# The per-layer embedding projections moved to the head of the first stage, and its small loads to GpSimd's queue

## The chip, the cores and the metric

The kernel runs on one core of a Trainium2 chip. The metric is the device time of one execution in microseconds. The core has five engines that each work through an instruction list of their own in order: PE (matrix products), DVE (vector), ACT (scalar), POOL (GpSimd) and SP (which only issues transfers). An instruction that has to wait for another engine or for a transfer holds everything behind it on its own engine. Transfers can be issued by SP, ACT and POOL.

## What is computed

Eleven stages in one launch, on 256 tokens of 1024 channels: an RWKV-7 mixer, an embedding gate, differential attention, a second embedding gate, a norm, then feed-forward, Mamba-2 and sliding-window layers. The change is in the first stage and in the preparation of the two embedding gates. Cut to these:

```python
h = x
# stage 1
hn = rms_norm(h, rw_norm);  dx = token_shift(hn) - hn
r, k, v, gate = ((hn + dx * mu[q]) @ w_in[q] for q in range(4))   # four 1024x1024 products
w_log = f(w0 + tanh((hn + dx * mu[4]) @ w1) @ w2)                 # low rank: w1 is 1024x64
a     = sigmoid(a0 + ((hn + dx * mu[5]) @ a1) @ a2)               # low rank: a1 is 1024x64
# delta rule over 256 tokens, 16 heads of 64; group norm with ln_w, ln_b; bonus; silu(gate)
h = h + y @ w_out
# stage 2 (and 4, with i = 1)
h = h + sigmoid(rms_norm(h, pe_norm[0]) @ pe_w_gate[0]) * (p[0] @ pe_w_proj[0])  # p[i]: 256x256, pe_w_proj[i]: 256x1024
```

The product `p[i] @ pe_w_proj[i]` depends on inputs alone, so it can be made at any time before its gate.

## The kernel before

Every float32 product is made as three: each operand is split into an upper part (a cast to a rounded float32, on ACT) and a lower part (the rest, a subtraction on DVE), and PE multiplies upper by upper, lower by upper and upper by lower. For weights, `wload` (L346) loads a block on SP's queue into a buffer `wr`, casts it into `wh` and subtracts into `wl`. There are few buffers, so that a later load waits for an earlier subtraction.

The first stage, `rwkv`, begins with `load_x` (L296), the sum of squares of the input on ACT, its root by POOL (`rsqrt`, L234), the normed input `hn` in four tiles on DVE (L213), and 16 transposes of it on PE (L229), whose results ACT evicts, scaled, into the tiles `hT`. The difference to the token before is `dx`. `mix` makes the operand of one projection from the two. Then come the value projection (8 blocks of weights) and beside it `lora`, the first low-rank products: they multiply `hT` and `dx` by the tile `wa`, which two transfers on POOL's queue fill (L934, from `rw_w1` and `rw_a1`), and by `wm`, which DVE makes from `wa`.

After the projections a scan works through four groups of four heads (`stream`): `pre` (decay, rate, keys), `scores`, `solve` and `post` (group norm, bonus, gate, and the transposes of the result). For each group `rows` (L709) loads five vectors and `pre` four small pieces of `rw_w2`, `rw_w0`, `rw_a2` and `rw_a0` (L720, L721), all on ACT's queue. Beside the groups run other pieces of work that fill PE: the gate projection, the output projection's halves `l0` and `l1` as far as groups are ready, and, from turn `FP` = 50 on, `ple_proj(0)` and `ple_proj(1)`, the two embedding projections. Each of these loads `p[i]` and transposes it, loads four blocks of 256 columns of `pe_w_proj[i]`, makes 12 products per block on PE, 96 in all for both, evicts each block on ACT and stores it to device memory from POOL's queue (L566). The tiles that hold the stored blocks are called `pp`; the stage `ple` loads them again.

The order of the instructions on each engine is set by a list scheduler that works from the program's order and the dependences. `late` keeps an instruction behind what its engine was given earlier in the program.

Of the kernel before, what the change touches and what calls it, by code (L numbers as in the profile page):

```python
# [8 lines left out]
F32 = mybir.dt.float32  # L9
# [12 lines left out]
NREF = 1  # refinements of the triangular solve  # L22
# banks of PSUM for short and for long use
# [12 lines left out]
# columns of the constant block  # L36
# [3 lines left out]
def constants():  # L40
    """Masks, the identity, rotary angles and distance buckets: from the shapes alone."""
# [18 lines left out]
    # reversed distance vector: column m holds the distance 255 - m; row 32 the mask outside the window  # L60
# [14 lines left out]
def weave(*gens):  # L75
    """Trace the generators by turns, a step each."""
    gens = list(gens)
    while gens:
        for g in list(gens):
            try:  # L80
                next(g)
            except StopIteration:
                gens.remove(g)
# [13 lines left out]
def par(*gens):  # L97
    """The generators by turns, as one generator."""
# [10 lines left out]
def spread(n, m, gen):  # L109
    """The generator's n steps over m turns."""  # L110
# [10 lines left out]
def spaced(n, *gens):  # L121
    """The generators one after another, n turns between."""
# [6 lines left out]
def when(cond, gen):  # L129
    """The generator, from the step on at which its condition holds."""  # L130
    while not cond():
        yield
    yield from gen
# [8 lines left out]
class Net:  # L142
    def __init__(self, ctx, tc, I, out, cst, dbg=None):
# [12 lines left out]
        self.ctx = ctx  # L156
        self.prologue(cst)
# [12 lines left out]
    def m(self, shape, dt=F32, tag="m", bufs=24):  # L170
        """Small tiles: those without a tag outlive a stage, the others do not."""
# [45 lines left out]
    def masked(self, out, a, b, least, init=3.0e38):  # L217
        """out = -(a + b), and its least element, not above init."""
# [12 lines left out]
    def rsqrt(self, out, a, scale, eps):  # L231
        """out = (a * scale + eps) ** -0.5"""
# [4 lines left out]
    def bc(self, vec, n):  # L237
        """A DRAM vector on every partition."""
# [7 lines left out]
    def late(self, ins):  # L246
        """Not before what its engine was given earlier: for loads and constants that need not be early."""
        self.tc.keep_in_program_order(ins)

# [1 line left out]
    def prologue(self, cst):  # L251
# [4 lines left out]
        nc.scalar.dma_start(self.cst, cst[:, :C_KEEP])  # L256
# [5 lines left out]
        # short vectors, on every partition  # L262
# [10 lines left out]

    def first_cols(self, names, queue):
        """Per-channel vectors, channels onto partitions."""
# [16 lines left out]
    def load_x(self, tile, early=False):  # L292
        """The input, as the residual so far."""
# [9 lines left out]
    def load_vec(self):  # L303
        for name, o in self.vec.items():
            self.nc.sync.dma_start(o, self.bc(self.I[name], o.shape[1]))
# [6 lines left out]
    def more_cols(self):  # L312
# [14 lines left out]
        # the gain of the final norm and of the first feed-forward norm after it  # L327
# [9 lines left out]
    def wload(self, W, k0, kn, n0, nn):  # L337
        """[128, kn, nn] of W as an upper and a lower part that sum to it exactly."""
# [12 lines left out]
        self.sub(l, r, h.bitcast(F32))  # L351
# [24 lines left out]
    def linear_cm_g(self, xT, K, W, n0, nn, evac):  # L376
        """The product with channels on partitions: evac takes two tiles of 128 channels by 256 tokens."""
# [16 lines left out]
    def linear2_g(self, xT, K, W, n0, evac):  # L394
        """256 columns, both token tiles side by side."""
# [22 lines left out]
    def split_g(self, src, ks, gains, outs):  # L418
        """src(t, k): [128 tokens, 128 channels]; appends channel-major pairs per gain."""
# [32 lines left out]
    def rstd(self):  # L452
        """Per-token 1/rms of the residual, [128, 2]."""
# [8 lines left out]
    def begin(self, gains):  # L462
        """The stage's input: per-token 1/rms and the residual, channel-major, times each gain."""
# [5 lines left out]
    def finish(self, l0, l1, gains):  # L469
        """The residual's two halves, and the next stage's input on the way."""  # L470
# [33 lines left out]
    def ffn(self, i, j, nxt, kv=False):  # L504
# [7 lines left out]
        def row():  # L512
            """1/rms as a row, on every partition."""
# [39 lines left out]
    def ple_proj(self, i):  # L553
        """p @ w_proj, kept in DRAM until its gate is known."""
# [35 lines left out]
    def final_norm(self):  # L590
        """The residual becomes its norm; what follows takes the operand from before it, the norm's
        gain and per-token factor folded in."""
# [959 lines left out]
```

## Time and profile before

| | us |
|---|---|
| three runs | 1570.53, 1572.88, 1576.21 |
| median | 1572.88 |
| span of the profiled execution, first to last instruction | 1568.3 |
| PE busy in it | 1525.5 |
| DVE busy | 1065.5 |
| ACT busy | 815.9 |
| POOL busy | 77.5 |

The profiled execution's own time is not given apart from its span; the span is 4.6 us below the median of the three runs, which is what lies around it and the difference between runs. Busy PE is modelled from its instructions' starts, so that a stretch that reads 100% busy can still hold gaps of a few per cent. A row of the timeline is: start in us, duration in us, engine, line, operation, result and operands, count, and in brackets the idle time before it with what ended it. Engine names with a q are the part of an engine that issues transfers.

### The profile page before, as it was taken

Reading aid. Unit: us, or ns where it says so; the run is one execution under the profiler, and the core shown is the slowest. Engines: PE = TensorE matmul, PEld = TensorE weight load, DVE = VectorE, ACT = ScalarE, POOL = GpSimd, SP = SyncE. Lnnn points to the kernel's source line nnn. Section 1 sums busy time; section 2 is a strip of 40 time slices with the busy share of each in tenths; the row PEclk is TensorE's granted clock in tenths of the full one; section 3 lists DMA queues with packets and bytes.
Section 4 is the critical chain, followed back from the end, with each engine's and each line's share of the span. In section 5 each row is a group of like instructions: output and inputs, shape, how many; then the busy total and the mean of one; then the engine's idle time right before and its main releaser. Section 6 shows DMA issues by size and latency. Waiting matters only on the chain.

```text
span 1568.3 us, 25792 instructions
## 1 busy us (share of the span) xinstructions
PE 1525.5 (97%) x10164; PEld 1349.5 (86%) x10164; DVE 1065.5 (68%) x1796; ACT 815.9 (52%) x1374; POOL 77.5 (5%) x79
## 2 busy tenths in 40 slices
PE   4999999999899999999999999999999999999998
PEld 4988988777678999887777899998999987799987
DVE  6887777876587756559877756665665657666563
ACT  3546546554466544447666744444544445654342
POOL 0000001111200000000000000000000002000000
PEclk9999999999999999999999999999999999999999
DMA  7421224566946554664442555465554653255463
GB/s 206 139 78 57 73 78 145 181 203 156 248 137 202 181 194 135 229 190 136 121 121 95 178 174 193 154 230 172 165 192 157 229 189 119 85 185 166 159 213 107
DMA packets 145500, 249.88 MB, mean 159 GB/s; under 512 B 11161, under 2 KB 42921, under 8 KB 145380
## 3 DMA queue, kind: packets, MB, share of 16 engines
q1 hardware_dynamic: 138420, 233.87, 46.4%
q0 software_dynamic: 3200, 10.81, 3.3%
q10 hardware_dynamic: 3760, 3.58, 0.9%
q8 instruction: 79, 1.29, 0.3%
q14 instruction: 41, 0.34, 0.1%
HBM read 242.16 MB, written 6.29 MB: 158 GB/s over the span
## 4 chain that ended last, share of the span: by engine, by line
PE 90%; DVE 4%; DMA 2%; ACT 2%; POOL 1%; issue 1%; ACTq 0%; POOLq 0%; DVEq 0%
PE pl L226 73%; PE ps L226 13%; PE ps L229 3%; DMA wr<-in_da_w_in_dram 1%; DVE wl L197 1%; DVE s L197 1%; DMA wa<-in_rw_w_dram 1%; DVE ac L209 1%; ACT s L223 0%; POOL s L993 0%; DVE s L209 0%; POOL m L234 0%; ACT h L223 0%; DMA wr<-in_rw_w_in_dram 0%; DMA base<-in_constants_dram 0%
## 5 line engine op out<-in xcount | busy, mean ns | idle before, releaser
L226 PE MATMUL pl<-wh,s 128*128 128x512 f32 (+1 forms) x2336 | 681.2, 370 | 6.2 <-ACT wh L223 3.2
L197 DVE TENSOR_TENSOR wl<-wr,wh 128x1024 fp32r<-128x1024 f32 (+1 forms) x460 | 528.5, 1173 | 123.0 <-ACT wh L223 121.7
L223 ACT ACTIVATE wh<-wr 128x1024 fp32r<-128x1024 f32 (+1 forms) x460 | 451.1, 1012 | 171.8 <-PE pl L226 103.3
L226 PE MATMUL pl<-s,wh 128*128 128x256 f32 x2816 | 509.1, 283 | 0.0
L226 PEld LDWEIGHTS pl<-wh,s 128*128 128x128 f32 x2336 | 422.3, 189 | 77.8 <-ACT wh L223 6.4
L226 PEld LDWEIGHTS pl<-s,wh 128*128 128x128 f32 x2816 | 439.5, 192 | 0.2
L226 PE MATMUL pl<-wl,s 128*128 128x512 f32 (+1 forms) x1168 | 430.2, 369 | 2.1 <-DVE wl L197 2.1
L226 PE MATMUL pl<-s,wl 128*128 128x256 f32 x1408 | 398.5, 283 | 0.0
L226 PEld LDWEIGHTS pl<-s,wl 128*128 128x128 f32 x1408 | 270.2, 192 | 0.0
L226 PEld LDWEIGHTS pl<-wl,s 128*128 128x128 f32 x1168 | 221.5, 190 | 36.0 <-DVE wl L197 3.3
L223 ACT ACTIVATE s<-s 128x512 f32<-128x512 f32 (+2 forms) x97 | 61.0, 629 | 209.7 <-DVE s L197 209.7
L197 DVE TENSOR_TENSOR s<-pl,s 128x512 f32<-128x512 f32 x44 | 30.4, 691 | 93.7 <-PE pl L226 93.7
L197 DVE TENSOR_TENSOR s<-pl,R 128x512 f32<-128x512 f32 x44 | 30.3, 691 | 82.8 <-PE pl L226 82.6
L234 POOL TENSOR_TENSOR m<-m,base 128x2 f32<-128x2 f32 (+2 forms) x25 | 24.2, 970 | 1006.9 <-DVE m L215 1006.9
L223 ACT ACTIVATE h<-ps 128x512 f16<-128x512 f32 x88 | 48.1, 600 | 36.9 <-PE ps L226 36.8
L223 ACT ACTIVATE s<-ps,base 128x256 fp32r<-128x256 f32 (+1 forms) x104 | 45.7, 471 | 25.0 <-PE ps L229 16.2
L209 DVE SCALAR_TENSOR_TENSOR s<-ps,base,s 128x256 fp32r<-128x256 f32 x96 | 43.6, 479 | 7.2 <-ACT s L223 6.1
L223 ACT ACTIVATE junk<-H 128x512 bf16<-128x512 f32 x40 | 25.1, 627 | 43.6 <-DVE H L209 29.2
L209 DVE SCALAR_TENSOR_TENSOR s<-s,s 128x512 f32<-128x512 f32 x56 | 38.4, 685 | 10.1 <-ACT s L223 9.4
L209 DVE SCALAR_TENSOR_TENSOR H<-pl,m,H 128x512 f32<-128x512 f32 x16 | 12.0, 751 | 47.1 <-PE pl L226 47.1
L226 PE MATMUL ps<-h,h 128*128 128x128 f16 x544 | 42.7, 220 | 1.3 <-ACT h L223 1.2
L226 PEld LDWEIGHTS <-h 128*128 128x128 f16 x576 | 34.9, 99 | 8.4 <-issue 4.8
(229 smaller groups left out, 1324.9 us busy)
## 6 DMA issues: line engine op xcount, KB each, us to landing
wr<-in_ffn_w_dram SPq DMA_DIRECT2D x248, 512.0 KB, 4.6
wr<-in_ssm_w_in_dram SPq DMA_DIRECT2D x40, 512.0 KB, 4.5
wr<-in_rw_w_in_dram SPq DMA_DIRECT2D x32, 512.0 KB, 4.7
wr<-in_da_w_in_dram SPq DMA_DIRECT2D x32, 512.0 KB, 4.7
wr<-in_pe_w_gate_dram SPq DMA_DIRECT2D x16, 512.0 KB, 4.3
wr<-in_ffn_w_dram SPq DMA_DIRECT2D x32, 256.0 KB, 3.1
wr<-in_ssm_w_out_dram SPq DMA_DIRECT2D x16, 512.0 KB, 3.8
wr<-in_rw_w_out_dram SPq DMA_DIRECT2D x8, 512.0 KB, 6.6
```

Source lines behind the costliest of these rows:

```text
L197: self.V.tensor_tensor(out=out, in0=a, in1=b, op=op)
L209: self.V.scalar_tensor_tensor(out=out, in0=a, scalar=sc, in1=b, op0=op0, op1=op1, **k)
L223: self.A.activation(out, a, f, **k)
L226: self.T.matmul(out, l, r, start=start, stop=stop)
L229: self.T.transpose(out, a, self.ident)
L234: self.G.tensor_tensor(out=out, in0=out, in1=self.mhalf[:, :out.free_size()].rearrange("p (a b) -> p a b", a=out.shape[1]) if len(out.shap ...
```

## The change

The two embedding projections are traced at the start of `rwkv`, right after `hn` and before its transposes, and no longer in the scan; the first four of their subtractions are kept in program order (`pin`). `rows` and the small pieces in `pre` are loaded on POOL's queue instead of ACT's. The eleven short vectors (`load_vec`) go from SP's queue to POOL's. The constants that are loaded first are half as many columns (384 instead of 768 of the block `base`), and the rest, with the level masks `lev`, is loaded on POOL's queue after `mix` of the values. The two multiplications that make `wm` are kept in program order.

```diff
 def prologue(self, cst):
-        nc.scalar.dma_start(self.cst, cst[:, :C_KEEP])
+        nc.scalar.dma_start(self.cst[:, :C_CAUS], cst[:, :C_CAUS])
...
+    def more_constants(self):
+        self.late(self.G.dma_start(self.cst[:, C_CAUS:], self.cdram[:, C_CAUS:C_KEEP]))
...
 def load_vec(self):
-            self.nc.sync.dma_start(o, self.bc(self.I[name], o.shape[1]))
+            self.late(self.G.dma_start(o, self.bc(self.I[name], o.shape[1])))
...
 def wload(self, W, k0, kn, n0, nn):
-        self.sub(l, r, h.bitcast(F32))
+        ins = self.V.tensor_tensor(out=l, in0=r, in1=h.bitcast(F32), op=ALU.subtract)
+        if self.pin:
+            self.pin -= 1
+            self.late(ins)
...
 def rwkv(self, nxt):
-        self.G.dma_start(lev[:, :7], self.cdram[:, C_LEV:C_LEV + 7 * P].rearrange("p (a b) -> p a b", a=7))
...
                 self.ts(o[:], self.H[t, f], r[:, t:t + 1], ALU.mult)
+
+        self.pin = 4
+        weave(self.ple_proj(0), self.ple_proj(1))
         for k0 in range(0, 8, 2):
...
         def lora():
-                self.mul(wm[:, :, q], wa[:, :, q], ...)
+                self.late(self.V.tensor_tensor(out=wm[:, :, q], in0=wa[:, :, q], ..., op=ALU.mult))
...
         def rows(tag, names, g):
-                nc.scalar.dma_start(o[:, j], ...)
+                self.G.dma_start(o[:, j], ...)
...
         def pre(g):
-                nc.scalar.dma_start(w2[at:at + 64, q], I[m][0, :, g * 256:(g + 1) * 256])
-                nc.scalar.dma_start(w2[one:one + 1, q], I[c0][:, g * 256:(g + 1) * 256])
+                self.G.dma_start(w2[at:at + 64, q], I[m][0, :, g * 256:(g + 1) * 256])
+                self.G.dma_start(w2[one:one + 1, q], I[c0][:, g * 256:(g + 1) * 256])
...
         weave(mix(2, *xv))
+        self.late(self.G.dma_start(lev[:, :7], ...))
+        self.more_constants()
...
         weave(after(FH, residual()), after(FG[0], spaced(FG[1], *[gate(g) for g in range(4)])),
-              after(FP, chain(self.ple_proj(0), self.ple_proj(1))), when(done(OP[0]), ...),
+              when(done(OP[0]), ...),
```

What this does to the order is seen in three places. The first is POOL's list at the start. Before, the two loads into `wa` stand right behind the root of the norm (the operation on the tile `m_22`):

```order
L628 DMA lev_8_95<-in_constants_dram 128x896
L234 ISA
L234 TENSOR_TENSOR m_22_114<-m_22_114,base_1_72 128x2
L934 DMA wa_6_91<-in_rw_w1_dram 128x8x64
L934 DMA wa_6_91<-in_rw_a1_dram 128x8x64
L283 DMA s_113_562<-in_da_norm_dram 8x128
```

After, the same stretch of POOL's list, from the root on:

```order
L235 TENSOR_TENSOR m_22_113<-m_22_113,base_1_72 128x2
L574 DMA pp0_147<-s_43_187 128x512
L574 DMA pp1_161<-s_48_203 128x512
L574 DMA pp0_147<-s_53_231 128x512
L574 DMA pp1_161<-s_58_247 128x512
L574 DMA pp0_147<-s_63_275 128x512
L574 DMA pp1_161<-s_68_291 128x512
L574 DMA pp0_147<-s_73_319 128x512
L574 DMA pp1_161<-s_74_322 128x512
L944 DMA wa_6_91<-in_rw_w1_dram 128x8x64
L944 DMA wa_6_91<-in_rw_a1_dram 128x8x64
L946 DMA lev_8_95<-in_constants_dram 128x896
```

The eight stores of the embedding projections, each of which waits for the eviction of its block, now stand between the root and the two loads into `wa`.

The second place is ACT's list behind the embedding projections. The tiles `s_68`, `s_73` and `s_74` are the last three evicted blocks, `s_9` to `s_12` are `hT`, and `s_81` is the first operand of the value projection. After:

```order
L224 ACTIVATE s_68_291<-pl_59_250 128x512
L224 ACTIVATE wh_94_400<-wr_93_399 128x1024
L224 ACTIVATE s_73_319<-pl_64_278 128x512
L224 ACTIVATE s_74_322<-pl_69_294 128x512
L224 ACTIVATE s_9_96<-ps_75_325,base_1_72 128x256 x2
L224 ACTIVATE wh_98_441<-wr_97_440 128x1024
L224 ACTIVATE s_10_97<-ps_76_334,base_1_72 128x256 x2
L224 ACTIVATE wh_103_484<-wr_102_483 128x1024
L224 ACTIVATE s_11_98<-ps_77_343,base_1_72 128x256 x2
L224 ACTIVATE s_12_99<-ps_78_352,base_1_72 128x256 x2
L224 ACTIVATE s_81_367<-b_80_364 128x512
```

Every eviction of `hT` now stands behind the last eviction of the embedding projections. On PE, 7 of the 96 embedding products stand ahead of the 16 transposes of `hn`, one among them and 88 behind them; behind those stands the first product with `wa`, ahead of the first value product:

```order
L227 MATMUL pl_69_294<-wh_71_296,s_33_143 128x256
L227 MATMUL pl_69_294<-wl_72_297,s_33_143 128x256
L227 MATMUL pl_69_294<-wh_71_296,s_34_144 128x256
L227 MATMUL ps_96_419<-s_9_96,wa_6_91 128x256
L227 MATMUL pl_92_398<-wh_94_400,s_81_367 128x256
```

The third place is the end of the scan on PE: the last products of the delta rule (`sa` by `GB`, and `S` by `qr`) and the transposes of the last group's result (`ps_851`). Before, 28 products of the output projection stand between the two; the first and the last of them are shown here with their neighbours:

```order
L226 MATMUL ps_841_3637<-S_31_162,qr_597_2700 128x128
L226 MATMUL ps_841_3637<-sa_840_3635,GB_636_2855 128x64 x2
L226 MATMUL pl_831_3601<-wl_844_3647,s_626_2823 128x512
L226 MATMUL pl_831_3601<-wh_843_3646,s_627_2824 128x512
L226 MATMUL pl_832_3602<-wh_843_3646,s_626_2823 128x512
```

```order
L226 MATMUL pl_814_3526<-wh_855_3707,s_810_3503 128x512
L226 MATMUL pl_815_3527<-wh_855_3707,s_809_3502 128x512
L226 MATMUL pl_815_3527<-wl_856_3708,s_809_3502 128x512
L229 MATMUL ps_851_3691<-base_1_72,s_798_3465 128x128 x4
L226 MATMUL pl_815_3527<-wh_855_3707,s_810_3503 128x512
```

After, none stands between them:

```order
L227 MATMUL pl_816_3531<-wh_855_3708,s_810_3512 128x512
L227 MATMUL pl_816_3531<-wl_856_3709,s_810_3512 128x512
L227 MATMUL pl_816_3531<-wh_855_3708,s_811_3513 128x512
L227 MATMUL ps_841_3638<-sa_840_3636,GB_676_3031 128x64 x2
L227 MATMUL ps_841_3638<-S_79_361,qr_645_2901 128x128
L227 MATMUL ps_841_3638<-sa_840_3636,GB_676_3031 128x64 x2
L230 MATMUL ps_851_3692<-base_1_72,s_804_3491 128x128 x4
L227 MATMUL pl_815_3530<-wh_858_3726,s_852_3697 128x512
```

These 28 products, and 4 that stood behind the transposes, moved up into the scan, to where the embedding products had been. From the start of the second stage on, PE's order is the same in both kernels.

## Rows read from the trace of the kernel before

**Rows 1.** The page: busy time with share and instructions, and the chain by engine

```profile
PE 1525.5 (97%) x10164; PEld 1349.5 (86%) x10164; DVE 1065.5 (68%) x1796; ACT 815.9 (52%) x1374; POOL 77.5 (5%) x79
...
PE 90%; DVE 4%; DMA 2%; ACT 2%; POOL 1%; issue 1%; ACTq 0%; POOLq 0%; DVEq 0%
```

**Rows 2.** Windows: busy us (instructions) of each engine, granted clock, DMA share, GB/s

```profile
20.00:30.00 10.00, 5.04 (x27) 4.89 (x28) 7.90 (x19) 3.77 (x9) 0.00 (x0) 0.66 0.62 179
...
200.00:250.00 50.00, 49.86 (x440) 43.52 (x439) 38.04 (x75) 26.27 (x49) 2.82 (x3) 1.00 0.26 86
250.00:290.00 40.00, 37.67 (x360) 33.97 (x360) 31.12 (x57) 25.25 (x45) 4.96 (x7) 1.00 0.40 131
```

**Rows 3.** Timeline of all engines from 13 to 25 us

```profile
13.74 1.03 POOL L934 DMA_DIRECT2D wa<-in_rw_w_dram  x1
...
13.81 2.29 DVE L213 TENSOR_SCALAR b<-x,m 128x512 f32<-128x512 f32 x4 [0.84 <-POOL m L234]
...
14.77 1.10 POOL L934 DMA_DIRECT2D wa<-in_rw_a_dram  x1
...
15.05 3.45 PE L229 MATMUL ps<-base,b 128*128 128x128 f32 x15 [0.23 <-DVE b L213]
...
16.39 2.20 ACTq L709 DMA_DIRECT2D row<-in_rw_r_k_dram  x1
...
20.82 1.57 ACT L223 ACTIVATE s<-ps,base 128x256 f32<-128x256 f32 x4 [0.70 <-DMA row<-in_rw_k_k_dram]
...
24.28 0.63 ACT L223 ACTIVATE s<-b 128x512 fp32r<-128x512 f32 x1 [1.90 <-DVE b L209]
...
24.96 1.19 PE L226 MATMUL ps<-s,wa 128*128 128x256 f32 x2 [6.46 <-ACT s L223]
```

**Rows 4.** Timeline of PE, two pairs of neighbouring 128x256 products after its restart

```profile
26.38 0.41 PE L226 MATMUL pl<-wh,s 128*128 128x256 f32 x1
26.59 0.41 PE L226 MATMUL pl<-wl,s 128*128 128x256 f32 x1
...
28.67 0.28 PE L226 MATMUL pl<-wl,s 128*128 128x256 f32 x1
28.79 0.28 PE L226 MATMUL pl<-wh,s 128*128 128x256 f32 x1
```

**Rows 5.** DMA issues: count, KB of each, median us from issue to landing

```profile
pp<-s POOLq DMA_DIRECT2D x8, 256.0 KB, 2.3
...
wa<-in_rw_w_dram POOLq DMA_DIRECT2D x1, 256.0 KB, 8.3
wa<-in_rw_a_dram POOLq DMA_DIRECT2D x1, 256.0 KB, 10.1
```

**Rows 6.** Groups by form, 195 to 290 us: busy us, mean ns, idle before

```profile
L223 ACT ACTIVATE wh<-wr 128x1024 fp32r<-128x1024 f32 x7 | 7.4, 1059 | 1.6 <-PE pl L226 1.6
L223 ACT ACTIVATE s<-pl 128x512 f32<-128x512 f32 x10 | 6.1, 606 | 2.2 <-PE pl L226 2.1
...
L566 POOL DMA_DIRECT2D pp<-s x8 | 4.5, 560 | 44.7 <-ACT s L223 37.6 <-ACT sa L223 7.1
```

**Rows 7.** Two of the lines' issues on ACT's queue: ns minimum/median/maximum, first and last start

```profile
L709 ACTq DMA_DIRECT2D row<-in_rw_k_k_dram x4: 334/355/366, 14.3 to 164.7; - x4
...
L720 ACTq DMA_DIRECT2D w<-in_rw_w_dram x4: 472/478/529, 2.2 to 119.2; - x4
```

**Rows 8.** Timeline of the end of the scan, 291 to 301 us

```profile
291.57 0.56 PE L226 MATMUL ps<-sa,GB 128*128 128x64 f32 x4
...
293.29 0.69 DVE L919 TENSOR_REDUCE m<-b 128x8 f32<-128x512 f32 x1 [0.70 <-ACT b L223]
...
294.33 1.67 POOL L234 TENSOR_TENSOR m<-m,base 128x8 f32<-128x8 f32 x1 [10.94 <-DVE m L215]
...
296.14 0.39 PE L226 MATMUL pl<-wl,s 128*128 128x512 f32 x1
...
296.82 0.39 PE L226 MATMUL pl<-wl,s 128*128 128x512 f32 x1
...
299.22 0.69 DVE L209 SCALAR_TENSOR_TENSOR s<-s,s 128x512 f32<-128x512 f32 x1
...
300.06 0.63 PE L229 MATMUL ps<-base,s 128*128 128x128 f32 x4 [1.50 <-DVE s L209]
```

More of the change, by code (lines that the diff above doesn't have):

```diff
@@ L156, in __init__ @@
         self.ctx = ctx
+        self.pin = 0
         self.prologue(cst)
@@ L673, in lora @@
             for q in range(2):
-                self.mul(wm[:, :, q], wa[:, :, q], self.colt[:, at + q * 8:at + q * 8 + 8].unsqueeze(2).broadcast_to([P, 8, 64]))
+                self.late(self.V.tensor_tensor(out=wm[:, :, q], in0=wa[:, :, q], in1=self.colt[:, at + q * 8:at + q * 8 + 8].unsqueeze(2).broadcast_to([P, 8, 64]), op=ALU.mult))
             ps = self.pq()
@@ L708, in rows @@
                 a = I[n]
-                nc.scalar.dma_start(o[:, j], bass.AP(tensor=a.tensor, offset=a.offset + g * 256, ap=[[0, P], [1, 256]]))
+                self.G.dma_start(o[:, j], bass.AP(tensor=a.tensor, offset=a.offset + g * 256, ap=[[0, P], [1, 256]]))
             return o
@@ L935, in rwkv @@
         weave(mix(2, *xv))
+        self.late(self.G.dma_start(lev[:, :7], self.cdram[:, C_LEV:C_LEV + 7 * P].rearrange("p (a b) -> p a b", a=7)))
+        self.more_constants()
         self.V.memset(state[:], 0.0)
@@ L951, in rwkv @@
         weave(after(FH, residual()), after(FG[0], spaced(FG[1], *[gate(g) for g in range(4)])),
-              after(FP, chain(self.ple_proj(0), self.ple_proj(1))), when(done(OP[0]), after(OP[1], chain(take(l0, OP[2]), take(l1, OP[3])))),
+              when(done(OP[0]), after(OP[1], chain(take(l0, OP[2]), take(l1, OP[3])))),
               *[after(n, stream(g)) for g, n in enumerate(ST)])
```

## The prediction, made before the changed kernel was run

> **What bounds the kernel now.** I read the page's busy times first, then its chain of waits, then windows of the two stretches that the change touches, and last the timeline at their edges. PE is busy for 97% of the span and carries 90% of the chain [rows 1], so work that leaves PE's list is worth its time on PE, provided nothing else ends later there. That holds in the scan: PE is busy for 49.86 of the 50 us from 200 to 250 and for 37.67 of the 40 us from 250 to 290 [rows 2], and the embedding projections lie there. The one long hole is at the start: the transposes of the normed input end at 18.5, and PE then stands idle for 6.46 us until 24.96 [rows 3]. The change puts the embedding products ahead of that hole. The question is whether they fill it, or whether what PE waits for in the hole is pushed back by them.
>
> What PE waits for has two strands. One is the operand: hn (DVE, from 13.81), transposes to 18.5, evictions into hT on ACT, the difference and the mix on DVE, the cast on ACT from 24.28 to 24.91. The other is the pair of loads into wa: issued at 13.74 and 14.77 [rows 3], landing 8.3 and 10.1 later [rows 5], so at 22.0 and 24.9. Both strands end at 24.9, and the profile names only one of them.
>
> **The start, after.** In PE's new list 88 of the 96 embedding products stand behind the transposes of hn, and hn needs the whole input. Neighbouring 128x256 products start 0.12 us apart at full clock and 0.21 us apart at half clock [rows 4]. If the transposes end at 18.5 as before, the last embedding product ends at 18.5 + 88 x 0.12 = 29.1 and its eviction (0.61, [rows 6]) at 29.7. The input shares its queue with fewer constants at first, so hn may come some 2 us earlier; I take the last eviction at 29, and 27 as the early end. The late end is half clock: 18.5 + 88 x 0.21 + 0.6 = 37.6. The granted clock was 0.66 on the mean from 20 to 30 us [rows 2], the 1.2 GHz level after the idle stretch; with products to run there is no such stretch, so I take full clock.
>
> From the last eviction both strands begin again. The operand: ACT's list has eight evictions into hT behind it (four took 1.57, so 3.1 in all), two casts of weights (1.06 each, [rows 6]) and the cast of the first mix (0.63) [rows 3]: 5.9 us, with DVE's share inside. The first value product therefore starts no earlier than 27 + 5.9 = 32.9, and at 34.9 from the middle value. The loads into wa: they stand behind all eight stores on POOL's list. The last store is issued at the last eviction plus 0.56 [rows 6], the two loads take 1.03 and 1.10 to issue [rows 3], so the second is issued at 29 + 0.56 + 1.03 = 30.6. Its landing is bounded by 2.3 us (256 KB stored from POOL's queue) and 10.1 us (the same load at the start, when the DMA engines were full) [rows 5]: 32.9 to 40.7. The weights of the value projection load in the same stretch, into buffers that come free late, so neither end fits; I take the middle, 6 us, and 36.6. Since the first product with wa stands ahead of the first value product on PE, all value work waits for the later of 34.9 and 36.6. PE restarts 11.7 us later than at 24.96, and what follows, up to the scan, is the same work. **Term 1: +11.7**, from +8 (operand, early) to +15.7 (loads, slow).
>
> A rule speaks for the lower end. The Trainium skill, DMA: Bandwidth & Descriptors, section "Anatomy of one DMA — SWDGE (gpsimd) path", gives a transfer from GpSimd's queue a fixed cost of about 2.0 us plus bytes over 436 GB/s, thus an estimate of 2.6 us for 256 KB. The stores agree with it (2.3), the loads into wa do not (8.3 and 10.1) [rows 5]. By it the second load lands at 33.2, the operand at 34.9 decides, and the sum is 1.7 us lower.
>
> **The scan, after.** It loses 96 x 0.12 = 11.5 us of products and about 1 us of transposes on PE, 12.5 in all; the 8 casts, 8 subtractions and 8 evictions go as well, on engines that wait for PE here. It gains 32 products of the output projection: 28 that stood ahead of the last transposes, and 4 behind them. Three such products start 0.68 us apart [rows 8], so 0.227 each, 7.3 us in all. The balance is -5.2 us where PE sets the pace throughout. PE had 2.3 us idle between 250 and 290 [rows 2], which no shorter list takes away, so I take -4.5, from -5.2 to -3. **Term 2: -4.5.**
>
> **The end of the scan, after.** The last group's result goes from the last product (ends 292.1) through an addition, a square, a reduction, POOL's root (1.67 us), five passes of DVE with a weight subtraction between, to the transposes at 300.06: 7.9 us [rows 8]. Before, 28 products, 6.4 us, covered it. These have moved up, so PE now stands idle for the 7.9 us. The loss is in term 2 already, which counts the moved products as added to the scan; what comes on top is the clock. After the hole at the start PE ran from 24.96 to about 28.6 at half clock, 3.6 us in which it did half the work [rows 3, 4]. **Term 3: +1.8**, from 0 to +1.8.
>
> **The queues.** 36 small loads leave ACT's queue (nine lines, four groups), 27 of them after the start, at 0.35 to 0.48 us each [rows 7]: some 11 us of an engine that is busy for 52% [rows 1] and mostly waits for PE. Where ACT's evictions hold PE's banks it helps; I take -1, from 0 to -4. On POOL these loads line up ahead of the small roots of the keys: after the value projection 5 loads of gains, 10 short vectors and 7 small pieces, about 0.53 each by the stores' 0.56 [rows 6], 12 us in which the first root isn't due yet; nothing. The late constants and level masks are needed only in the scan; nothing, and if they came late the first group's scores would wait for their landing, at most the 10.1 of the slowest load. The short vectors move off SP's queue, where they stood between weight loads that wait for buffers; nothing. **Term 4: -1.**
>
> **The sum** is 11.7 - 4.5 + 1.8 - 1 = +8.0 us. Against the profiled span of 1568.3 that is 1576.3; the median of the runs is 4.6 above the span, so I forecast 1572.9 + 8 = 1581.
>
> **Rivals.** About 0.3%, 4.7 us, is what a measurement of this kernel can tell from no change.
> *The loads into wa land at once* (2.3 to 2.6 us, as the stores and the named rule have it) and the input comes early: PE restarts at 33 to 33.5, +8.3. With the full -5.2 in the scan, +1 of clock and -1.5 on ACT the sum is +2.6: 1575.5, within 0.3%. For it: DMA engines are free once the buffers for weights are full. Against it: the same loads took 8.3 and 10.1.
> *The embedding products end before the hole* (the other side). The point from which it decides is the last eviction: at 22 or before, the restart comes at 28, +3, and with -5.2 in the scan and -3 on ACT the sum is -5.2: 1567.7, faster. It needs hn's transposes to end at 11 or all but a few products to run ahead of them. Against it: 88 stand behind, and hn came at 13.81 when the input was first in the queue.
> *Half clock at the start.* PE waits for weights, casts and subtractions between its products, the granted clock falls as it did between 20 and 30 us [rows 2], and the last eviction comes at 34 to 37.6: restart at 42 to 45, +17 to +20, with terms 2 to 4 1586 to 1590.
>
> **How the numbers follow.** Forecast as worked out (restart at 34.5 to 41): 0.50. Loads at once: 0.22. Ends before the hole: 0.13. Half clock: 0.15. The forecast's own times run from 1577.6 to 1586 (restart +9.5 to +16, the other terms within their bounds). So faster by over 0.3%: 0.13; within 0.3%: 0.24, the second case and the low edge of the first; slower: 0.63. The range leaves out the third case and the top of the fourth: 1572 to 1590.
>
> **What would show it.** In the profile after, look at the first product with wa on PE: I expect it between 34.5 and 41, released by the load into wa or by the cast of the mix. The eight stores must stand ahead of the two loads on POOL's timeline, the evictions into hT behind the last eviction from 27 to 30. At the scan's end PE must show an idle time of 7 to 8 us ahead of the last transposes. The distance from the restart to the scan's last product should be some 4 to 6 us shorter than the 266.6 before (24.96 to 291.57). A restart at 28 or earlier would make the prediction wrong on the fast side, one at 45 on the slow side; a gain in the middle of more than 6 us would say that ACT's queue cost more than I think.

## The result, and the profile after

The changed kernel takes 1588.12 us (median of four runs, 1587.89 to 1589.88) beside 1572.80 for the kernel before: a ratio of 1.0095, 95% interval 1.0080 to 1.0110. That is 15.3 us slower, 7 more than the forecast of 1581. It lies inside the range of 1572 to 1590, but above the forecast's own times, which end at 1586. One execution of a later run, the one with products held in order, took 3826 us and is left out of its figures. The profiled executions stand 17.6 us apart (1568.3 and 1585.9): runs here lie some 2 us above their spans, which makes the profiled execution of before its quickest, so differences of a us or two between stretches of the two traces are not read as anything.

The page of the changed kernel, busy times and chain, answers to [rows 1]: the busy shares hardly differ, POOL has the 48 added issues, and in the chain PE falls from 90 to 88%, while DMA, issue and POOL have a point more each.

```profile
PE 1533.5 (97%) x10164; PEld 1353.2 (85%) x10164; DVE 1065.4 (67%) x1796; ACT 808.8 (51%) x1374; POOL 102.2 (6%) x127
...
PE 88%; DVE 4%; DMA 3%; issue 2%; POOL 2%; ACT 1%; POOLq 0%; DVEq 0%; ACTq 0%
```

The timeline of the start of the changed kernel, all engines, answers to [rows 3]:

```profile
11.05 0.72 POOL L235 TENSOR_TENSOR m<-m,base 128x2 f32<-128x2 f32 x1 [4.20 <-DVE m L216]
...
14.12 0.69 DVE L198 TENSOR_TENSOR s<-ps,s 128x512 fp32r<-128x512 f32 x1 [3.15 <-ACT s L224]
...
15.33 1.67 DVE L214 TENSOR_SCALAR b<-x,m 128x512 f32<-128x512 f32 x4
...
17.41 2.37 PE L230 MATMUL ps<-base,b 128*128 128x128 f32 x14
...
22.03 0.61 POOL L574 DMA_DIRECT2D pp<-s  x1 [10.25 <-ACT s L224]
...
30.51 1.31 ACT L224 ACTIVATE s<-pl 128x512 f32<-128x512 f32 x2 [0.65 <-ACT wh L224]
...
32.12 0.54 POOL L574 DMA_DIRECT2D pp<-s  x1 [0.18 <-issue]
...
32.59 0.69 DVE L198 TENSOR_TENSOR s<-s 128x510 f32<-128x510 f32 x1 [1.47 <-ACT s L224]
...
33.74 0.90 POOL L944 DMA_DIRECT2D wa<-in_rw_a_dram  x1
...
37.08 0.84 ACT L224 ACTIVATE s<-ps,base 128x256 f32<-128x256 f32 x2 [1.18 <-DMA pp<-s]
37.81 0.63 ACT L224 ACTIVATE s<-b 128x512 fp32r<-128x512 f32 x1
...
41.62 1.19 PE L227 MATMUL ps<-s,wa 128*128 128x256 f32 x2 [10.48 <-DMA wa<-in_rw_a_dram]
```

The last of the eight stores is issued at 32.12, the second load into `wa` at 33.74, and PE restarts at 41.62 on its landing. The first operand had been ready at 38.44, so the loads account for the last 3.2 of the 10.48 us of idle time and the operand's strand for the rest. PE was at full clock until 31 us; what kept it idle was not its clock.

The issues of the changed kernel, KB and median us to landing, beside [rows 5]: the stores land later than before (2.3), the loads a little sooner than before (8.3 and 10.1).

```profile
pp<-s POOLq DMA_DIRECT2D x8, 256.0 KB, 5.7
wa<-in_rw_w_dram POOLq DMA_DIRECT2D x1, 256.0 KB, 7.3
wa<-in_rw_a_dram POOLq DMA_DIRECT2D x1, 256.0 KB, 7.7
```

The windows of the changed kernel (columns as in [rows 2]: stretch, length, busy PE, PEld, DVE, ACT, POOL, granted clock, DMA share, GB/s):

```profile
20.00:30.00 10.00, 10.00 (x79) 9.45 (x78) 3.57 (x6) 6.79 (x12) 3.30 (x6) 1.00 0.89 292
30.00:40.00 10.00, 1.14 (x10) 0.94 (x8) 8.50 (x16) 6.62 (x13) 4.00 (x6) 0.79 1.06 366
40.00:50.00 10.00, 8.38 (x43) 7.98 (x44) 10.00 (x22) 3.79 (x5) 0.00 (x0) 0.69 0.61 185
...
290.00:300.00 10.00, 5.44 (x42) 4.25 (x41) 6.62 (x13) 1.68 (x3) 2.44 (x3) 0.59 0.11 26
300.00:310.00 10.00, 9.80 (x58) 7.98 (x56) 4.76 (x10) 3.18 (x5) 0.00 (x0) 0.89 0.48 152
310.00:320.00 10.00, 2.25 (x7) 1.64 (x8) 5.63 (x9) 1.23 (x2) 1.66 (x1) 0.62 0.86 321
320.00:330.00 10.00, 10.00 (x48) 8.24 (x47) 6.60 (x14) 6.66 (x17) 1.12 (x2) 0.87 0.17 52
```

PE's timeline at the end of the scan, answering to [rows 8], shows two long waits where the kernel before had 0.96 and 1.50 us. The first is ahead of the third group's transposes, the second ahead of the last group's:

```profile
295.57 1.08 PE L230 MATMUL ps<-base,s 128*128 128x128 f32 x4 [4.56 <-DVE s L210]
...
309.25 0.56 PE L227 MATMUL ps<-sa,GB 128*128 128x64 f32 x4
317.07 1.09 PE L230 MATMUL ps<-base,s 128*128 128x128 f32 x4 [7.26 <-DVE s L210]
```

The wait of 0.96 us, in the kernel before:

```profile
280.81 0.63 PE L229 MATMUL ps<-base,s 128*128 128x128 f32 x4 [0.96 <-DVE s L209]
```

Fixed points are needed to compare stretches of the two executions. POOL's square roots are the same instructions in both kernels, eight in the scan and the ninth in the next stage's norm, so their starts divide the execution. The table gives the length of each stretch in us, with PE's busy time in brackets. The sixth root starts at 226.23 before and at 243.29 in the changed kernel, the ninth at 309.75 and at 328.88:

| stretch | before | changed | difference |
|---|---|---|---|
| start to PE's restart | 24.96 | 41.62 | +16.7 |
| restart to first root | 53.14 (53.09) | 54.22 (54.17) | +1.1 |
| first to sixth root | 148.13 (146.94) | 147.45 (146.57) | -0.7 |
| sixth to ninth root, which held the embedding products | 83.52 (79.56) | 85.59 (72.33) | +2.1 |
| ninth root to the end | 1258.5 | 1257.0 | -1.5 |

Nearly the whole loss is at the start, and the stretch that lost 96 products got no shorter. Its window in the kernel before and in the changed one, with a clock of 1.00 and of 0.88:

```profile
226.23:309.75 83.52, 79.56 (x674) 69.97 (x674) 63.45 (x115) 49.12 (x92) 9.45 (x12) 1.00 0.48 161
```

```profile
243.29:328.88 85.59, 72.33 (x565) 59.18 (x566) 56.31 (x104) 39.06 (x73) 7.26 (x7) 0.88 0.31 104
```

PE is busy for 7.2 us less there and waits 13.3 us instead of 4.0. And the 12.5 us of products that left show as only 7.2: some 5 us came back (79.56 - 12.5 = 67.1 against 72.33). They are found behind the two waits. From the third group's transposes to the scan's last product PE has the same work in both kernels, and it takes 13.68 us at a granted clock of 0.76 instead of 10.76 us at 1.00. From the last transposes to the ninth root it takes 11.81 us at 0.77 instead of 9.69 at 1.00, with four products fewer. That is 5.0 us together.

### The profile page after: what moved, and what is told of

Its sections match the earlier page's. It is cut to its first block, busy times and chain, and to the rows that moved or that the text cites. A ratio compares the mean times of both kernels' runs of the same rounds, so it can differ in the third digit from the quotient of the medians.

```text
span 1585.9 us, 25825 instructions
## 1 busy us (share of the span) xinstructions
PE 1533.5 (97%) x10164; PEld 1353.2 (85%) x10164; DVE 1065.4 (67%) x1796; ACT 808.8 (51%) x1374; POOL 102.2 (6%) x127
## 4 chain that ended last, share of the span: by engine, by line
PE 88%; DVE 4%; DMA 3%; issue 2%; POOL 2%; ACT 1%; POOLq 0%; DVEq 0%; ACTq 0%
PE pl L227 72%; PE ps L227 13%; PE ps L230 3%; DMA wr<-in_da_w_in_dram 2%; DVE wl L356 1%; DVE s L198 1%; DVE ac L210 0%; DMA wa<-in_rw_a_dram 0%; POOL m L235 0%; POOL s L1005 0%; DVE s L210 0%; ACT s L224 0%; ACT junk L224 0%; DMA w<-in_rw_w_dram 0%; POOL m L1387 0%
## 5 line engine op out<-in xcount | busy, mean ns | idle before, releaser
L224 ACT ACTIVATE wh<-wr 128x1024 fp32r<-128x1024 f32 (+1 forms) x460 | 444.7, 1009 | 88.8 <-PE pl L227 56.5
L230 PE MATMUL ps<-base,s 128*128 128x128 f32 x200 | 34.0, 287 | 17.8 <-DVE s L210 12.2
L230 PEld LDWEIGHTS ps<-base,s 128*128 128x128 f32 x200 | 25.2, 148 | 24.7 <-issue 14.2
L210 DVE SCALAR_TENSOR_TENSOR s<-s,s 128x512 f32<-128x512 f32 x56 | 38.4, 686 | 10.1 <-ACT s L224 9.4
```

The source lines that it names most:

```text
L210: self.V.scalar_tensor_tensor(out=out, in0=a, scalar=sc, in1=b, op0=op0, op1=op1, **k)
L224: self.A.activation(out, a, f, **k)
L230: self.T.transpose(out, a, self.ident)
```

## The experiments

The theory was that the move costs what it puts ahead of PE's restart, and that the scan gives some of it back. The rivals concern what sets the restart, and whether the scan gives anything back.

**The two halves of the change.** First the move of the projections alone, with all loads on the queues of before:

```diff
+        self.pin = 4
+        weave(self.ple_proj(0), self.ple_proj(1))
...
-              after(FP, chain(self.ple_proj(0), self.ple_proj(1))), when(done(OP[0]), ...),
+              when(done(OP[0]), ...),
```

`pin` keeps the first four subtractions in program order, as in the changed kernel.

> The kernel before with one thing changed: the embedding projections are traced at the head of the stage (their first four subtractions kept in order); small loads, short vectors, constants and level masks stay on their old queues and places. My theory, that the whole loss comes from where the projections stand (the loads into wa and the evictions into hT wait behind them; the last two groups' transposes lose the products that covered their waits): PE restarts at 40 to 43 us, idle times of 4 to 5 and of 7 to 8 us stand ahead of the last two groups' transposes, and the time is 13 to 18 us above before, about that of the changed kernel. Rival, that the loads moved to GpSimd's queue carry a good part of the loss: at most 8 us above before.

Measured: 1594.3 us, ratio 1.0129 [1.0114, 1.0144], worse than the whole change and outside both expectations: the two waits in the scan are as the theory has them (4.52 and 7.22 us), but the restart is later than its 40 to 43 us and the time 21 us above before instead of 13 to 18. PE's timeline of this kernel: the restart is 6 us later than the changed kernel's.

```profile
47.69 0.77 PE L227 MATMUL ps<-s,wa 128*128 128x256 f32 x1 [9.74 <-DMA wa<-in_rw_a_dram]
```

On SP's queue the short vectors stand here between the embeddings and their weights (the second load of an embedding is issued at 11.12, the first weights at 11.96), and the first store follows at 27.48 instead of 22.03. ACT's first cast of these weights stands behind the small loads on ACT's own queue and starts at 18.18 instead of 12.97; which of the two queues decides was not separated. So the other half of the change, the queues, belongs to the move: it makes the move cheaper. Then everything but the move:

```diff
-        self.pin = 4
-        weave(self.ple_proj(0), self.ple_proj(1))
...
-              when(done(OP[0]), ...),
+              after(FP, chain(self.ple_proj(0), self.ple_proj(1))), when(done(OP[0]), ...),
```

> The changed kernel with the embedding projections back in the scan: small loads, short vectors, late constants and level masks on GpSimd's queue, and the multiplications for wm in order. My theory: these cost nothing, and the eviction of hT no longer waits behind loads that ACT issues, so PE restarts at 22 to 25 us and the time is from 3 us below before to 1 us above. Rival, that GpSimd's queue is the cost: 6 us or more above before, with waits of DVE for short vectors or of PE for the small roots between 60 and 100 us.

Measured: 1570.37 us, ratio 0.9979 [0.9970, 0.9989]. As the theory has it, PE's first product with `wa` starts at 21.99, without a wait for it. But the first root starts at 79.3, against 78.1 before, so an earlier restart doesn't by itself bring what follows forward. The runs put the gain at some 3 us, below the 4.7 us that the prediction takes as the limit of what can be told from no change; the two profiled executions are only 0.7 us apart, so the trace doesn't show where it comes from. This is the quickest kernel of the study.

**What the products cost in the scan.** The kernel before with the products left out: the eight stores write zeros, and the two gates add nothing.

```diff
-        p = self.s()
...
-        yield from self.split_g(lambda t, k: pv[:, t, k * P:(k + 1) * P], (0,), (None,), outs)
+        z = self.s()
+        self.late(self.V.memset(z[:], 0.0))
...
-            def ev(ps, g=g):
-                o = self.s()
-                self.act(o[:], ps[:])
-                self.G.dma_start(scr[g], o[:])
-            yield from self.linear2_g(outs[0], 2, I["pe_w_proj"][i], g * 256, ev)
+            self.G.dma_start(scr[g], z[:])
+            yield
```

> The kernel before with the embedding projections left out: no loads of p and of its weights, no casts, subtractions, products and evictions; the eight stores remain and write zeros, so the two gates add nothing. It measures what the projections cost in the scan. My theory: they filled waits of the delta rule and let the output projection's products stay behind to cover the last two groups' waits, so that leaving them out is worth little: 0 to 4 us below before, with the same two idle times ahead of the last two groups' transposes. Rival, on which the second term of my prediction rested, that PE paces the scan: 9 to 12 us below before.

Measured: 1573.7 us, ratio 0.9999 [0.9990, 1.0009], as the theory has it and some 9 us away from the rival. Work that PE is busy with for 12.5 us costs nothing measurable. PE's timeline and the window from the sixth to the ninth root show why: the same two waits open as in the changed kernel, and the stretch is 86.9 us long, 3.4 more than with the products.

```profile
280.70 1.09 PE L229 MATMUL ps<-base,s 128*128 128x128 f32 x4 [4.39 <-DVE s L209]
301.01 1.09 PE L229 MATMUL ps<-base,s 128*128 128x128 f32 x4 [7.23 <-DVE s L209]
...
226.90:313.80 86.90, 73.30 (x573) 60.24 (x572) 58.54 (x107) 40.04 (x76) 8.02 (x8) 0.90 0.31 104
```

So it isn't the new place that opens the waits but the absence of the products from the old one.

**Half of the move.** One embedding's projection at the start, the other's in the scan:

```diff
-        weave(self.ple_proj(0), self.ple_proj(1))
+        weave(self.ple_proj(0))
...
-              when(done(OP[0]), ...),
+              after(FP, self.ple_proj(1)), when(done(OP[0]), ...),
```

> The changed kernel with the first embedding's projection (48 of the 96 products, four of the eight stores) ahead of the first strand's mix and the second's back in the scan, at the step where the kernel before has both. Runs so far give 1570.4 us with both in the scan and 1588.1 us with both ahead; the run without the products (1573.7, the kernel before 1573.4 beside it) says that they cost the scan nothing. Theory (each product ahead of the mix costs its own time there, since TensorE, the evictions and VectorE's mix run behind one another, and the scan gives nothing back as its last groups wait for VectorE): about half way, 1576 to 1582 us; the loads into wa are issued at 26 to 29 us, VectorE begins its mix at 24 to 28 us instead of 32.6, and the square root of the first group comes at 85 to 89 us (both in the scan 79.3, both ahead 95.8). The two waits before the last transposes are between the one kernel's 1.0 and 1.5 us and the other's 4.6 and 7.3. Rival (the cost is a fixed one of the loads into wa standing behind stores on POOL's queue, whatever their number): 1584 to 1588 us. Other rival (48 products fit into TensorE's idle time at the start, and only the second 48 cost): within 2 us of 1570.4 us.

Measured: 1583.15 us (1581.02 to 1584.8), ratio 1.0062 [1.0049, 1.0076], 1 us above the theory's range (1576 to 1582) and below the rival's (1584 to 1588). The start is nearly as the theory has it: `wa` is issued at 25.09 and 26.00 (expected from 26 on), DVE begins its mix at 25.02, the first root stands at 86.29, 7.0 us behind the kernel with none ahead (79.3) and 9.5 before the one with all (95.84). The missing part is at the end. The expectation put the two waits between those of the two kernels; the first is (2.52), the second is not. It is open in full, though half the products are there, and the stretch from the sixth to the ninth root is the longest of all, 88.65 us:

```profile
31.72 1.19 PE L227 MATMUL ps<-s,wa 128*128 128x256 f32 x2 [7.44 <-DMA wa<-in_rw_a_dram]
...
290.78 0.63 PE L230 MATMUL ps<-base,s 128*128 128x128 f32 x4 [2.52 <-DVE s L210]
311.00 1.09 PE L230 MATMUL ps<-base,s 128*128 128x128 f32 x4 [7.25 <-DVE s L210]
```

With 96, 48 and 0 products that stretch takes 83.5, 88.7 and 85.6 us. Its length doesn't follow PE's work. Why the half is the longest was not followed up.

**What the open waits cost.** The changed kernel with the first output product of each block kept in program order, which puts 29 of them back ahead of the last transposes:

```diff
-        self.T.matmul(out, l, r, start=start, stop=stop)
+        return self.T.matmul(out, l, r, start=start, stop=stop)
...
-                    self.mm(o, xh, wh[:, j, :nn], start=(k == 0), stop=False)
+                    ins = self.mm(o, xh, wh[:, j, :nn], start=(k == 0), stop=False)
+                    if self.hold_l and not (t or j):
+                        self.late(ins)
...
+        self.hold_l = 1
...
+        self.hold_l = 0
```

`hold_l` is 1 from the scan to the end of the first stage.

> The changed kernel, with one thing kept in program order: the first output-projection product of each block, so that 29 of these products stand on TensorE ahead of the last group's four transposes and some 67 between the third group's and the last's (changed kernel: 0 and 24; kernel before: 28 and 52). Nothing of the start is touched: TensorE restarts at 41.6 us as before. Theory (the tail's uncovered waits cost time): the wait of 7.26 us before the last transposes falls under 1.5 us, the one of 4.56 us before the third group's stays, the stretch behind keeps the full clock, and the kernel gains 5 to 8 us on the changed one: 1580 to 1583 us. Rival (covering a wait is worth nothing, since the covering products only move, as the run without the embeddings' projections suggests): within 2 us of the changed kernel, 1586 to 1590 us.

Measured: 1584.36 to 1587.48 us in four runs, with a median of 1585.5, ratio 1.0078 [1.0064, 1.0092] against 1.0095 for the changed kernel; the profiled execution is 3.5 us shorter (1582.4), and its stretch from the sixth to the ninth root is 3.4 us shorter (82.2). The last wait closes as planned, the first hardly:

```profile
291.07 1.08 PE L231 MATMUL ps<-base,s 128*128 128x128 f32 x4 [3.55 <-DVE s L211]
315.44 0.63 PE L231 MATMUL ps<-base,s 128*128 128x128 f32 x4 [1.27 <-DVE s L211]
...
260.00:270.00 10.00, 8.15 (x72) 7.62 (x71) 4.27 (x9) 2.79 (x6) 0.00 (x0) 0.73 0.18 53
290.00:300.00 10.00, 8.93 (x52) 7.04 (x53) 6.50 (x13) 2.14 (x3) 0.92 (x2) 0.74 0.13 28
```

Its time lies between the theory's range (1580 to 1583) and the rival's (1586 to 1590), and the mechanism is neither's: the products taken for the last wait are missing earlier, where small waits appear and the clock is lower (0.73 from 260 to 270 us, where the changed kernel has 1.00). The intervals overlap, so the gain itself, 2 to 3.5 us, is not certain. Covering one wait at the cost of others is worth at most some quarter of the loss.

**What sets the restart.** If the loads into `wa` are the limit, then issuing them first should bring the restart forward to the operand's 38.4, some 3 us:

```diff
+        for q, n in enumerate(("rw_w1", "rw_a1")):
+            self.late(self.G.dma_start(wa[:, :, q], I[n][0].rearrange("(k p) n -> p k n", p=P)))
...
-        for q, n in enumerate(("rw_w1", "rw_a1")):
-            self.late(self.G.dma_start(wa[:, :, q], I[n][0].rearrange("(k p) n -> p k n", p=P)))
         weave(mix(2, *xv))
```

> The changed kernel with the two loads into wa issued first on GpSimd's queue. Theory, that the stores ahead of them decide the restart of PE: the operand's strand (cast of the first mix, which ended at 38.4 in the changed kernel) ends last instead, PE restarts at 38 to 39 us, and the time is 3 us below the changed kernel, so 11 to 13 us above before. Rival, that the half MB of these loads delays the input and the weights of the embedding projections by as much: PE restarts at 41 or later and nothing is gained.

Measured: 1628.14 us, ratio 1.0341 [1.0319, 1.0363], 40 us above the changed kernel, which neither expectation had. The restart does come, at 34.08 and so 4 us ahead of the theory's 38, but the first root comes only at 95.4 (95.84 without), and 37 us are lost behind the scan (from the ninth root to the end 1294.4 against 1257.0). There the loads of weights wait. SP's row of this kernel, and the same instructions in the changed one:

```profile
309.24 30.18 SPq L351 DMA_DIRECT2D wr<-in_pe_w_gate_dram  x6
```

```profile
305.09 4.33 SPq L351 DMA_DIRECT2D wr<-in_pe_w_gate_dram  x6
```

The buffers are shared out automatically from the memory that is left. In this kernel `wa` lives from the start; the share-out falls to 3 raw and 3 upper weight buffers, where the changed kernel has 8 and 7. Whether those buffers are the loss was tried by itself, with the order of the changed kernel and an unused tile:

```diff
+        pad = self.c([P, 6144], F32, "pad")
+        self.V.memset(pad[:, 0:1], 0.0)
```

> The changed kernel with an unused tile of 24 KB on each partition added (and one element of it set): the order of all engines is the changed kernel's, but the automatic allocation has only 3 raw and 3 high-part weight buffers left in the main part, against 8 and 7. It is a control for the run that issued the loads into wa first, which was 38 us slower than the changed kernel and had 3 of each too. Theory (that loss was the buffers'): the restart stays at 41.6 us, weight loads wait for free buffers from 300 us on, and the kernel takes 1615 to 1635 us. Rival (the loss came from the early loads or the order): 1586 to 1592 us.

Measured: 1629.89 us, ratio 1.0360 [1.0346, 1.0374], as the theory had it. The restart comes at 42.56, 0.9 us later than in the changed kernel, on the same load, and SP shows the same row:

```profile
42.56 1.19 PE L227 MATMUL ps<-s,wa 128*128 128x256 f32 x2 [10.98 <-DMA wa<-in_rw_a_dram]
...
313.73 30.13 SPq L353 DMA_DIRECT2D wr<-in_pe_w_gate_dram  x6
```

So the loss of the run with the loads first is the buffers'. The same scarcity of buffers costs 7.5 us before the first root, which starts at 103.38 here and at 95.84 in the changed kernel. This makes the unused tile the kernel to compare early loads with, as both have 3 raw and 3 upper buffers. POOL's first root in the kernel with the loads first, and in the one with the unused tile:

```profile
95.42 1.79 POOL L769 TENSOR_TENSOR m<-m,base 128x8 f32<-128x8 f32 x1
```

```profile
103.38 1.68 POOL L769 TENSOR_TENSOR m<-m,base 128x8 f32<-128x8 f32 x1
```

Beside it, early loads bring the first root forward by 8.0 us, the ninth by 4.4 (332.26 against 336.63), and the end by 1.8 us, which the intervals of the two runs don't tell from nothing. Early loads were tried again with 7 to 9 buffers of each kind, by taking the stores off POOL's queue:

```diff
-                self.G.dma_start(scr[g], o[:])
+                self.nc.scalar.dma_start(scr[g], o[:])
```

> The changed kernel with the eight stores of the embeddings' products issued on ACT's queue instead of POOL's, so that the two loads into wa stand right behind the square root on POOL and are issued at some 15 us rather than 33 us. The automatic buffer allocation leaves 7 to 9 buffers for raw and for converted weights, near the changed kernel's. Theory (the loads into wa are what TensorE waits for at its restart, and nothing else is far behind them): the restart falls from 41.6 to 37 to 39 us, now set by ACT's evictions and the first strand's mix (last eviction 31.8 us, first operand ready at about 38.4 us), and the kernel is some 3 us below the changed one, 1584 to 1586 us. Rival (ACT's own issues put its evictions back by as much as the loads gain): restart at 41 us or later, 1588 us or more. A third reading concerns the earlier run that issued these loads first and lost 38 us: if early loads themselves were the loss, it comes here too (1620 us); if its three weight buffers were, it does not.

Measured: 1591.5 us, ratio 1.0118 [1.0102, 1.0133], no faster than the changed kernel, though the restart is 5.3 us earlier. Neither theory had both. Timeline of this kernel:

```profile
35.26 0.60 ACT L224 ACTIVATE s<-pl 128x512 f32<-128x512 f32 x1 [2.36 <-DMA pp<-s]
...
36.27 8.33 PE L227 MATMUL ps<-s,wa 128*128 128x256 f32 x24 [3.51 <-ACT s L224]
36.61 0.69 DVE L198 TENSOR_TENSOR s<-s 128x510 f32<-128x510 f32 x1 [1.85 <-ACT s L224]
```

ACT's last eviction waits for the landing of a store, so that the evictions into `hT` end later and DVE begins its mix at 36.61 instead of 32.59. PE starts earlier and then waits 3.4 us for lower parts from DVE, which reads 10.00, 10.00 and 9.78 us busy from 50 to 80. Of 5.3 us, 2.0 are left at the first root (93.83) and none at the third (159.58 against 158.84). So the loads are the last of PE's waits at the restart, but DVE's mix ends hardly earlier. How much early loads alone would give with these buffers was not isolated, as this kernel delays the mix itself.

**The products behind the mix.** The last way to spare the start: the projections traced after the mix of the values, so that `wa` and `hT` come first.

```diff
-        self.pin = 4
-        weave(self.ple_proj(0), self.ple_proj(1))
...
         weave(mix(2, *xv))
+        weave(self.ple_proj(0), self.ple_proj(1))
```

> The changed kernel with the embeddings' projections traced behind the first strand's mix and the loads into wa: on TensorE the first product with wa comes first, then the 96 products, then the value products; on POOL the loads into wa stand ahead of the eight stores; on ACT the first strand's evictions stand ahead of the projections' four. The products stay out of the scan, so that the two waits of 4.6 and 7.3 us near its end stay uncovered. Theory (what the change loses is the place of the products ahead of the restart, their evictions and stores, at 16.7 us, while taking them out of the scan gains nothing): the chain to the first value product shortens to 32 to 35 us, and the kernel takes 1577 to 1582 us. Rival (the products cost the same wherever they stand at the start, since TensorE runs them one after the other): restart of the value products at 40 us or later and 1586 to 1589 us.

Measured: 1593.01 us, ratio 1.0127 [1.0113, 1.0140]. The first product with `wa` starts at 19.89, but the 96 products run from 24.18 to 48.2, and the value products come behind them. The timeline of PE and two windows of this kernel:

```profile
24.18 1.10 PE L227 MATMUL pl<-wh,s 128*128 128x256 f32 x2 [3.51 <-ACT wh L224]
32.35 0.58 PE L227 MATMUL pl<-wl,s 128*128 128x256 f32 x1 [7.07 <-DVE wl L356]
...
20.00:30.00 10.00, 1.77 (x4) 0.74 (x4) 10.00 (x24) 3.79 (x7) 0.00 (x0) 0.52 0.10 32
30.00:40.00 10.00, 7.65 (x45) 7.65 (x46) 6.47 (x13) 2.59 (x5) 1.09 (x2) 0.63 0.62 192
```

Now the lower parts of their weights wait behind DVE's mixes, and PE, idle for 7.07 us, starts at half clock. The first root stands at 98.27. The rival held for the restart, and the time is above even its range: neither place tried at the start has room for 96 products in PE's idle time.

## Why the prediction came out as it did

**Sign and place** were right: slower, by a late restart of PE behind eviction, stores and loads into `wa`, with nothing lost on the queues. The size was short, 8 of the 15.3 us. The total lies beyond the forecast's own times, in the band that the prediction gave to half clock at the start (1586 to 1590), which did not happen. That the range holds it is in part luck: it was wide enough for another cause.

**Term 1, the start: 16.7 us where the sum had 11.7**, just past its late end of +15.7, and a restart at 41.6 just past the expected 34.5 to 41. The chain was the predicted one, and most of its links were longer. The last eviction ends at 31.8, not 29: the sum let `hn` come 2 us earlier, and it came 1.5 us later (15.33 against 13.81), its 16 transposes ending at 19.8. The norm's root did come 2 us earlier (11.05 against 13.05). But ahead of `hn` on DVE's list stand subtractions of the embeddings, and the first of them waited for ACT until 14.12; this the prediction did not look at. From 19.8 on 88 products took 11.3 us, 0.13 each (0.12 in the sum). The second load was issued 1.9 us behind the last eviction (1.6 in the sum), and it landed after 7.75, not the chosen 6. The landing is the term of this sum that was mis-sized: the middle was taken between a store's 2.3 and the load's 10.1 on the ground that neither end fitted. But the loads of the value weights kept the DMA engines full (share 1.06 at 366 GB/s from 30 to 40 us), so the rows of the same load were the nearer ones. The Trainium skill's rule (DMA: Bandwidth & Descriptors, "Anatomy of one DMA — SWDGE (gpsimd) path"), an estimate of 2.6 us for 256 KB, fits neither these loads nor the stores in this traffic (5.7).

**Term 2, the scan: -4.5 expected, +1.0 measured** from the restart to the scan's last product (267.63 against 266.61), which the prediction wanted 4 to 6 us shorter, term 4 included. This is the step whose mechanism failed. The sum read a busy PE (37.67 of 40 us, [rows 2]) as a PE that sets the pace, and balanced 12.5 us of products leaving against 7.3 arriving. The predicted wait of some 7.9 us ahead of the last transposes is there (7.26). But a second one of 4.56 us opened ahead of the third group's transposes, where the kernel before waits 0.96; there 20 products, 15 of the output projection and 5 of the embeddings, had covered 4.4 us (275.47 to 279.85). That place was not looked at. And behind both waits the clock was lower. The run without the products says it directly: where they stood, they were worth nothing that can be measured (ratio 0.9999). They filled time in which PE would otherwise have waited for DVE.

**Term 3, the clock: named, and too small.** The sum had +1.8 behind the last transposes, where it measured 2.1 us with four products fewer. Behind the third group's transposes, where the sum had nothing, it is 2.9 us more, which lie within the +1.0 of term 2. Half clock behind the hole at the start did not go away either, as the sum's lower end allowed: from 40 to 50 us the mean clock is 0.69.

**Term 4, the queues: right in sign, and near its far end.** Taken at -1 with an end of -4; the kernel with all but the move is 3.3 us faster [1.7, 4.7]. No engine waited for late constants or short vectors in the changed kernel. What the sum didn't see is that beside the move the same edits are worth more: 5.3 us by the ratios (1.0129 against 1.0095).

**The rivals.** Loads that land at once are refuted by the 7.75. Products that end before the hole are refuted by the last eviction, which ends at 31.8. Half clock at the start came near in its numbers (restart at 42 to 45, total 1586 to 1590), but PE ran at full clock from 20 to 31 us, and the late restart has another cause.

**Open** is what early loads into `wa` would give with buffers and mix left as they are; with few buffers they gave 8 us at the first root and some 2 at the end, which is within the noise. Not tried was a kernel in which `hn` stands ahead of the embeddings' subtractions on DVE.

## What to carry to other kernels

Work that an engine does while it would otherwise wait can cost nothing, as the 12.5 us of products did here: ask of the work to be moved which wait would open without it, at every place where it or its substitutes stand, and not whether the engine reads busy. A move to an idle stretch can pay only if its whole chain, from the input it needs to the stores and the loads behind them on the same queue, fits into that stretch. And before an order of loads is judged by its time, see whether the share-out of buffers is still the same.

## What the runs showed that was not expected

An unused tile of 24 KB per partition cost 42 us, by leaving 3 raw weight buffers instead of 8 and 3 upper ones instead of 7: six loads of weights were held for 30 us of SP's time instead of 4. A reordering of two loads of 256 KB did the same without any tile being added. And the waits of PE in the scan were paid a second time: the four transposes behind those of 3.55, 4.39, 4.56, 7.23, 7.25 and 7.26 us took 1.08 to 1.09 us, with products at half clock after them, and the same four behind 0.96, 1.27, 1.50 and 2.52 us took 0.63 [rows 8].
